# Values of branch B carried by the 512-column products of branch A in a hybrid attention encoder layer

## The chip, the cores and the metric

The kernel runs on one core of a Trainium2 chip. A core has a tensor engine (PE; its weight loads are listed apart as PEld), a vector engine (DVE), a scalar engine (ACT), a GpSimd engine (POOL) and a sync engine (SP) that here only issues DMAs; ACT and POOL issue DMAs too. Each works through its own instruction stream in order and waits on semaphores for the others. The metric is the device time of one execution in microseconds; the figure for a kernel is the median of its runs.

## The reference

One encoder layer is applied to two inputs with the same weights: `x_prompt` of 1024 tokens and `x_sample` of 512, both with a model width of 1024. Branch A is grouped-query attention (8 query heads, 2 key/value heads, 64 wide, queries and keys normalised and rotated), branch B neighbourhood attention on a token grid (8 heads, 64 wide).

```python
z = xn @ w_in                     # xn = rmsnorm(x) * g
qa, ka, va, qb, kb, vb, ga, gb = jnp.split(z, idx, axis=-1)   # 512,128,128,512,512,512,1024,1024
qa = rope(rmsnorm(qa, q_norm_g)); ka = rope(rmsnorm(ka, k_norm_g))
o_a = gqa_attention(qa, ka, va)
o_b = neighbourhood_attention(qb, kb, vb, rpb)
merged = sigmoid(ga) * (o_a @ w_proj_a) + sigmoid(gb) * (o_b @ w_proj_b)
h = x + merged @ w_out
y = rmsnorm(h + relu(rmsnorm(h) @ w_mlp_up)**2 @ w_mlp_down)
```

All is float32. The columns that matter here are `qa` (0 to 512), `ka` (512 to 640), `va` (640 to 768) and `vb` (1792 to 2304) of `w_in`.

## The kernel before

**Precision by three products.** A float32 product is made of three products of a faster type. Every operand is split into a high part (an ACT copy into that type) and a low part (a DVE subtraction of the copy from the source); `split` (L182 to L191) does it for weights, and `mm3` (L194 to L197) multiplies high by high, high by low and low by high into one accumulator. A product over the 1024 rows of the weights takes eight blocks of 128 rows, so 24 matrix instructions per 128 tokens.

**Two trunks, one after the other.** Trunk 0 is `x_sample` (4 token tiles of 128, `first` is true), trunk 1 is `x_prompt` (8 token tiles). In each trunk a loop over `g` (0 and 1), the head groups of branch A, runs a projection stage `phR` and an attention stage `phA`; then come branch B, the output projection and the MLP, which hold most of the time.

**The projection stage.** For each token tile `tt`:
- product `z`: 384 columns, which are the 256 of four query heads of group g, 64 of its key head and 64 of its value head. Its weights come from `load_a(g)` (L456): two loads of 512 KB for the queries, one raw tile for keys and values, split into `wh` and `wl`, tiles of 4 x 384 columns. The very first tile of trunk 0 is multiplied in two parts, 256 and 128 columns.
- `values(tt - 2)` (L606): product `zv` of 256 columns, the values of four heads of branch B (heads 0 to 3 with g = 0, 4 to 7 with g = 1). ACT copies the high part to `vt`, DVE subtracts the low part (L616, L617), and a DMA from ACT's queue stores 256 KB to `vd` in memory (L620), from where branch B gathers its key rows later. The weights `wv` come from `load_v(g)`, two loads of 512 KB; those for g = 1 are loaded and split during the attention stage of g = 0.
- `heads_t(tt - 2)` (L585): three transposes by PE (L590) of the rotated query and key heads `rr`; ACT and DVE write the high and low parts into `qT` and `kT` (L594 to L599).
- `chain(tt)` (L623): ACT squares the five heads (L629, into a scratch tile `sq`) and copies the value's high part (L630); DVE makes the mean (L176); POOL takes the power (L180); DVE the value's low part (L632) and the scaled heads `t` (L637); POOL `u` (L645); DVE `t` (L651) and `rr` (L653), with one head of `rr` on POOL (L654).

With g = 0 the token tiles are also normalised and transposed in this stage (`xn`, `ptxs`, L260 to L306). The tiles `z` and `zv` are made in accumulators of one pool; `raw` tiles, in which weights land before they are split, come from a pool of their own, and SP issues their loads in order, each waiting for its tile to come free.

**The tail of a projection stage** (after the last `z`): `values(NT - 2)`, `heads_t(NT - 2)`, `values(NT - 1)`, six steps of `fill.pull`, `heads_t(NT - 1)`. `fill` is a store of matrix work with no urgent reader, the gate products `gpss` of 512 columns: one step is three matrix instructions. The attention stages draw from the same store between their own instructions.

**Order.** Within a stage a scheduler orders the instructions of each engine; `keep_in_program_order` pins some. The stages follow one another in the order written.

Of the kernel before, what the change touches and what calls it, by code (L numbers as in the profile page):

```python
# [18 lines left out]
P = 128  # L19
# [42 lines left out]
def encoder(ctx: ExitStack, tc: tile.TileContext, xs, outs, w):  # L62
# [333 lines left out]
    def run(tr, nxt, first):  # L396
# [59 lines left out]
        def load_a(g, between=None, then=None, last=None):  # L456
            wh, wl, rq = [], [], []
            for kb in range(2):
                wh.append(slot([P, 4, 384], F32R, f"wgh{N}_{g}_{kb}"))
                wl.append(slot([P, 4, 384], F32R, f"wgl{N}_{g}_{kb}"))  # L460
                raw = rawp.tile([P, 1024], F32, tag="raw", name=f"rawq{N}_{g}_{kb}")
                rv = raw.rearrange("p (k c) -> p k c", c=256)
                nc.sync.dma_start(
                    rv,
                    win[kb * 512 : (kb + 1) * 512, 256 * g : 256 * g + 256].rearrange("(k p) c -> p k c", p=P),
                )
                rq.append(rv)
# [9 lines left out]
            for i, off in enumerate((512 + 64 * g, 640 + 64 * g)):  # L477
                nc.sync.dma_start(
                    rv[:, :, 64 * i : 64 * i + 64],
                    win[:, off : off + 64].rearrange("(k p) c -> p k c", p=P),  # L480
                )
            if last is not None:
                last()
            for kb in range(2):
                split(
                    wh[kb][:, :, 256:384],
                    wl[kb][:, :, 256:384],
                    rv[:, kb * 4 : kb * 4 + 4, :],
                    between is not None,
                )  # L490
            return wh, wl

        def load_v(g, alloc, pin=False, hold=None):
            return load_cols(win, 1792 + 256 * g, 256, f"v{N}_{g}", alloc, pin, hold)

        early = {}
        for g in range(2):
            with phase(f"phR{N}_{g}") as ph:
                xn_of, pre = {}, {}
                fresh = g == 0 and tr.ready < NT  # L500
                if fresh and not first:

                    def shape(tag):
                        bufs, dims, dt = {
                            "vt": (2, [P, 4, P], F32R),
                            "sq": (1, [P, 5, HD], F32),
                            "rt": (3, [P, 2, HD], F32),
# [5 lines left out]

                    pre = {tag: shape(tag) for tag in ("vt", "sq", "rt", "t", "u", "rr")}
                    gb = ph.tile([P, 1, D], F32, tag="gb", name=f"gb{N}", bufs=1)
# [52 lines left out]
                if g == 0 and first:  # L568
                    setup_tables()
                if early:  # L570
                    wv = early.pop("v")
                elif fresh and not first:
                    wv = load_v(g, lambda s_, d_, n_: room.pop(0))
                else:
                    wv = load_v(g, lambda s_, d_, n_: ph.tile(s_, d_, tag="wv", name=n_, bufs=2), first and fresh, held)
                qT = [slot([P, 2, T], F32R, f"qT{N}_{g}_{i}") for i in range(2)]
# [29 lines left out]
                def values(tt):  # L606
# [5 lines left out]
                    for k in range(NC8):  # L612
# [6 lines left out]
                    pending.append(  # L619
                        lambda: nc.scalar.dma_start(vd[tt * P : (tt + 1) * P, 4 * g : 4 * g + 4, :], vt.bitcast(F32))  # L620
                    )

                def chain(tt, z, rt):  # L623
                    nm = f"{N}_{g}_{tt}"
                    sq = pre.pop("sq", None) or ph.tile([P, 5, HD], F32, tag="sq", name=f"sq{nm}", bufs=1)
                    zq = z[:, :320].rearrange("p (h d) -> p h d", d=HD)
                    ss = sml.tile([P, 8], F32, tag="ss", name=f"ssA{nm}")
                    for i in range(5):
                        nc.scalar.activation(sq[:, i, :], zq[:, i, :], AF.Square, accum_out=ss[:, i : i + 1])  # L629
                    nc.scalar.activation(vhl[:, tt, 0:HD], z[:, 320:384], AF.Copy)  # L630
                    r = rstd(ss[:, :5], 5, HD, f"A{nm}")
                    nc.vector.tensor_tensor(  # L632
                        vhl[:, tt, HD:P], z[:, 320:384], vhl[:, tt, 0:HD].bitcast(F32), op=ALU.subtract
                    )
                    t = pre.pop("t", None) or ph.tile([P, 5, HD], F32, tag="t", name=f"t{nm}", bufs=2)
                    for i in range(5):
# [21 lines left out]
                for tt in range(NT):  # L658
# [18 lines left out]
                    if first and fresh and tt < 2:  # L677
                        tc.keep_in_program_order(op)
                    z = mm(f"z{nm}")[:, :384]
                    js = slice(j * P, (j + 1) * P)  # L680

                    for c0, c1 in ((0, 256), (256, 384)) if first and g + tt == 0 else ((0, 384),):
                        for k in range(NC8):
# [11 lines left out]
                    if tt >= 2:  # L695
                        values(tt - 2)
                        heads_t(tt - 2)
# [30 lines left out]
            with phase(f"phA{N}_{g}") as ph:  # L728
# [1067 lines left out]
```

## Time and profile before

| | us |
|---|---|
| three runs | 2144.89, 2145.60, 2146.26 (median 2145.6) |
| profiled execution | 2146.21, of which the traced span is 2144.4 |
| PE busy | 2115.7 (99% of the span) |
| DVE, ACT, POOL busy | 1474.8, 1112.1, 368.7 |
| phR of trunk 0, g = 0 and g = 1 | about 8 to 54 and 97 to 131 |
| phR of trunk 1, g = 0 and g = 1 | about 378 to 454 and 583 to 648 |

How to read the rows: `zs<-wghs,xs_0h` is an instruction that writes tile z from the weights wgh and the activations xs_0h (buffer numbers left out); L196 is the line of the kernel before. In the timeline the first number is the start in us from the beginning of the span, the second the duration; xN means N instructions put together, and a bracket at the end gives the idle time of the engine just before and what ended it. Matrix instructions overlap in the pipeline, so the pace of PE is read from start to start and not from durations. In the list of waits a row gives the engine and line that waited, what for, the us in total, how many times, and the longest. In the table by stage a row gives the stretch, its length, the busy us of PE, PEld, DVE, ACT and POOL with the number of instructions, PE's granted clock, the share of the DMA engines and GB/s.

### The profile page before, as it was taken

To read this page: it belongs to the slowest core of one execution; us is meant where nothing else is said; L and a number is where in the kernel's file an instruction comes from. 1 tells how busy PE (TensorE), PEld (TensorE's weight loads), DVE (VectorE), ACT (ScalarE), POOL (GpSimd) and SP (SyncE) were. 2 spreads that over 40 slices of the span, in tenths; PEclk is the share of its full clock that TensorE was granted. 3 is DMA by queue.
4 is the path that set the end of the run, shared out by engine and by line. 5 is a ranking of instruction groups with operands and counts; after the bars stand their busy time and mean duration, and the time that the engine had idled before them with its cause. 6 is when DMAs were issued, how large, how long until landed. Compare 5 with 4: busy or idle time off the path is not lost.

```text
span 2144.4 us, 32035 instructions
## 1 busy us (share of the span) xinstructions
PE 2115.7 (99%) x10967; PEld 1847.5 (86%) x10967; DVE 1474.8 (69%) x2889; ACT 1112.1 (52%) x2367; POOL 368.7 (17%) x470
## 2 busy tenths in 40 slices
PE   8999999999999999999999999999999999999998
PEld 7788778888898888887888899999999988888886
DVE  6675786877667755656882877777777777759563
ACT  5655654557646644555530566566655643434342
POOL 3232310433233223333200200003000000000000
PEclk9999999999999999999999999999999999999999
DMA  6437557520122133444472665578545799688561
GB/s 185 130 105 206 152 160 253 179 84 25 54 79 71 42 95 109 131 119 112 140 236 105 213 195 183 173 247 205 165 142 156 256 357 341 212 280 278 165 204 61
DMA packets 321258, 354.07 MB, mean 165 GB/s; under 512 B 31551, under 2 KB 255431, under 8 KB 321095
## 3 DMA queue, kind: packets, MB, share of 16 engines
q1 hardware_dynamic: 277927, 279.65, 41.8%
q10 hardware_dynamic: 36016, 52.19, 7.0%
q0 software_dynamic: 7152, 20.19, 3.5%
q8 instruction: 87, 1.43, 0.3%
q14 instruction: 76, 0.62, 0.1%
HBM read 264.85 MB, written 87.88 MB: 164 GB/s over the span
## 4 chain that ended last, share of the span: by engine, by line
PE 76%; DVE 1%; issue 0%; ACT 0%; POOL 0%; POOLq 0%; ACTq 0%; DVEq 0%
PE dn L196 6%; PE dn L197 6%; PE dn L195 6%; PE pTs L783 3%; PE gpss L195 3%; PE gpss L197 3%; PE gpss L196 3%; PE ua L197 2%; PE ua L195 2%; PE ua L196 2%; PE ud L195 2%; PE ud L197 2%; PE ud L196 2%; PE uc L197 2%; PE uc L195 2%; PE uc L196 2%
## 5 line engine op out<-in xcount | busy, mean ns | idle before, releaser
L197 PE MATMUL dn<-wd,al 128*128 128x512 f32 x624 | 242.8, 389 | 0.0
L196 PE MATMUL dn<-wd,ah 128*128 128x512 f32 x624 | 242.8, 389 | 0.0
L195 PE MATMUL dn<-wd,ah 128*128 128x512 f32 x624 | 242.7, 389 | 0.0
L1273 ACT ACTIVATE ah<-ar 128x512 fp32r<-128x512 f32 x168 | 104.3, 627 | 205.8 <-PE dn L196 183.6
L1274 DVE TENSOR_TENSOR al<-ar,ah 128x512 fp32r<-128x512 f32 x168 | 113.8, 685 | 77.8 <-ACT ah L1273 65.9
L195 PEld LDWEIGHTS dn<-wd,ah 128*128 128x128 f32 x624 | 117.1, 188 | 24.4
L196 PEld LDWEIGHTS dn<-wd,ah 128*128 128x128 f32 x624 | 117.1, 188 | 24.3
L197 PEld LDWEIGHTS dn<-wd,al 128*128 128x128 f32 x624 | 117.1, 188 | 24.2
L789 DVE TENSOR_TENSOR ptls<-pTs,pths 128x512 fp32r<-128x512 f32 x160 | 107.6, 686 | 37.9 <-ACT pths L788 37.0
L749 POOL TENSOR_SCALAR ps<-ps,rls 128x1024 f32<-128x1024 f32 (+1 forms) x96 | 97.1, 1012 | 212.6 <-DVE rls L748 192.1
L788 ACT ACTIVATE pths<-pTs 128x512 fp32r<-128x512 f32 x160 | 94.2, 598 | 73.8 <-PE pTs L783 71.6
L743 DVE TENSOR_REDUCE nms<-ss 128x1 f32<-128x1024 f32 (+1 forms) x96 | 99.8, 1041 | 25.3 <-PE ss L741 24.8
L195 PE MATMUL gpss<-xs_0h,w_gs 128*128 128x512 f32 x256 | 105.5, 412 | 0.5 <-DVE ot_Bs L440 0.4
L180 POOL TENSOR_TENSOR rs_f<-ms_f,mhalf 128x1 f32<-128x1 f32 x6 | 4.0, 667 | 590.7 <-DVE ms_f L176 590.7
L746 ACT ACTIVATE ps<-ss,nms 128x1024 f32<-128x1024 f32 (+1 forms) x96 | 93.3, 973 | 22.5 <-DVE nms L743 18.7
L783 PEld LDWEIGHTS pTs<-ident,ps 128*128 128x128 f32 x640 | 78.1, 140 | 28.2 <-POOL ps L749 4.3
L197 PE MATMUL gpss<-xs_0h,w_gs 128*128 128x512 f32 x256 | 101.1, 395 | 0.3 <-DVE w_gs L190 0.3
L196 PE MATMUL gpss<-xs_0l,w_gs 128*128 128x512 f32 x256 | 101.0, 394 | 0.0
L783 PE MATMUL pTs<-ident,ps 128*128 128x128 f32 x640 | 98.9, 274 | 1.3 <-DVE ptls L789 0.6
L1273 ACT ACTIVATE A<-S 128x512 fp32r<-128x512 f32 x128 | 75.8, 623 | 31.8 <-DVE S L1336 23.0
L957 POOL TENSOR_TENSOR bms<-rects,msks 128x384 f32<-128x384 f32 (+1 forms) x72 | 70.2, 978 | 128.7 <-DVE nmbs L974 107.5
L1274 DVE TENSOR_TENSOR A<-S,A 128x512 fp32r<-128x512 f32 x128 | 84.5, 686 | 4.1 <-ACT A L1273 4.1
(330 smaller groups left out, 6372.1 us busy)
## 6 DMA issues: line engine op xcount, KB each, us to landing
ar<-ud SPq DMA_DIRECT2D x120, 512.0 KB
br<-in_w_mlp_down_dram SPq DMA_DIRECT2D x72, 512.0 KB
rawu<-in_w_mlp_up_dram SPq DMA_DIRECT2D x64, 512.0 KB
ud<-c ACTq DMA_DIRECT2D x128, 192.0 KB
raw_gs<-in_w_in_dram SPq DMA_DIRECT2D x32, 512.0 KB
zgs<-sgs ACTq DMA_DIRECT2D x48, 256.0 KB
ud<-cs SPq DMA_DIRECT2D x64, 192.0 KB
raw_os<-in_w_out_dram SPq DMA_DIRECT2D x16, 512.0 KB
```

Of the source, the lines that this page charges most:

```text
L195: nc.tensor.matmul(out, ah, bh, start=start, stop=False, **kw)
L196: nc.tensor.matmul(out, ah, bl, start=False, stop=False, **kw)
L197: nc.tensor.matmul(out, al, bh, start=False, stop=stop, **kw)
L743: nc.vector.tensor_reduce(nm_, s, axis=AX.X, op=ALU.max, negate=True)
L746: nc.scalar.activation(p, s, AF.Exp, bias=nm_, accum_out=l)
L749: nc.gpsimd.tensor_scalar(p, p, rl, 1.0, op0=ALU.mult, op1=ALU.mult)
L783: nc.tensor.transpose(pt[:, j * P : (j + 1) * P], PP[u, j][:, kc * P : (kc + 1) * P], ident)
L788: nc.scalar.activation(hi, pt, AF.Copy)
L789: nc.vector.tensor_tensor(lo, pt, hi.bitcast(F32), op=ALU.subtract)
L957: nc.gpsimd.tensor_tensor(bm.rearrange("p (r c) -> p r c", c=32), rects[h][:, ir : ir + kr_n, jr : jr + 32], msk[:, hf * 3 + ct, :].rearra ...
L1273: nc.scalar.activation(hi, src, AF.Copy)
L1274: nc.vector.tensor_tensor(lo, src, hi.bitcast(F32), op=ALU.subtract)
```

## The change

Each 512-column accumulator is filled: the product `z` gets 128 further columns, the values of two heads of branch B. With g = 0 these are heads 0 and 1, with g = 1 heads 6 and 7 (`VB`). The other four heads (2 to 5) are made by `values`, once per trunk, in the stage of g = 0.

- `load_a` loads and splits a fourth piece (128 columns, 512 KB, `rawvb`), so `wh` and `wl` are 512 wide. In the first call it gets a slot of its own; in the other calls it takes a raw tile.
- `load_v` is called once per trunk. The load and split of value weights in the attention stage of g = 0 is gone; the fourth piece of `load_a(1)` is loaded there.
- `chain` copies and subtracts the two value heads into `vz` (one buffer with g = 0, two with g = 1) and stores 128 KB from ACT's queue. Its squares are written into `t` instead of a scratch tile.
- The first tile's two parts are 256 and 256 columns.
- The tail with g = 0 is as before. With g = 1, where there are no `values`, three steps of gate products stand ahead of `heads_t(NT - 2)` and six ahead of `heads_t(NT - 1)`.

```diff
         def load_a(g, between=None, then=None, last=None):
...
-                wh.append(slot([P, 4, 384], F32R, f"wgh{N}_{g}_{kb}"))
-                wl.append(slot([P, 4, 384], F32R, f"wgl{N}_{g}_{kb}"))
+                wh.append(slot([P, 4, 512], F32R, f"wgh{N}_{g}_{kb}"))
+                wl.append(slot([P, 4, 512], F32R, f"wgl{N}_{g}_{kb}"))
...
+            raw = raw_tile(f"rawvb{N}_{g}") if between is None else slot([P, 1024], F32, f"rawvb{N}_{g}", True)
+            rb = raw.rearrange("p (k c) -> p k c", c=P)
+            off = 1792 + HD * VB[g]
+            op = nc.sync.dma_start(rb, win[:, off : off + P].rearrange("(k p) c -> p k c", p=P))
+            if between is not None:
+                tc.keep_in_program_order(op)
...
+            for kb in range(2):
+                split(
+                    wh[kb][:, :, 384:512],
+                    wl[kb][:, :, 384:512],
+                    rb[:, kb * 4 : kb * 4 + 4, :],
+                    between is not None,
+                )
             return wh, wl

-        def load_v(g, alloc, pin=False, hold=None):
-            return load_cols(win, 1792 + 256 * g, 256, f"v{N}_{g}", alloc, pin, hold)
+        def load_v(alloc, pin=False, hold=None):
+            return load_cols(win, 1792 + 2 * HD, 256, f"v{N}", alloc, pin, hold)
+        VB = (0, 6)
...
-                            "sq": (1, [P, 5, HD], F32),
+                            "vz": (1, [P, 2, P], F32R),
...
-                if early:
-                    wv = early.pop("v")
-                elif fresh and not first:
-                    wv = load_v(g, lambda s_, d_, n_: room.pop(0))
-                else:
-                    wv = load_v(g, lambda s_, d_, n_: ph.tile(s_, d_, tag="wv", name=n_, bufs=2), first and fresh, held)
+                if fresh and not first:
+                    wv = load_v(lambda s_, d_, n_: room.pop(0))
+                elif g == 0:
+                    wv = load_v(lambda s_, d_, n_: ph.tile(s_, d_, tag="wv", name=n_, bufs=2), first and fresh, held)
...
-                        lambda: nc.scalar.dma_start(vd[tt * P : (tt + 1) * P, 4 * g : 4 * g + 4, :], vt.bitcast(F32))
+                        lambda: nc.scalar.dma_start(vd[tt * P : (tt + 1) * P, 2:6, :], vt.bitcast(F32))
...
                 def chain(tt, z, rt):
-                    sq = pre.pop("sq", None) or ph.tile([P, 5, HD], F32, tag="sq", name=f"sq{nm}", bufs=1)
+                    t = pre.pop("t", None) or ph.tile([P, 5, HD], F32, tag="t", name=f"t{nm}", bufs=2)
...
-                        nc.scalar.activation(sq[:, i, :], zq[:, i, :], AF.Square, accum_out=ss[:, i : i + 1])
+                        nc.scalar.activation(t[:, i, :], zq[:, i, :], AF.Square, accum_out=ss[:, i : i + 1])
                     nc.scalar.activation(vhl[:, tt, 0:HD], z[:, 320:384], AF.Copy)
+                    vz = pre.pop("vz", None) or ph.tile([P, 2, P], F32R, tag="vz", name=f"vz{nm}", bufs=1 + g)
+                    zb = z[:, 384:512].rearrange("p (h d) -> p h d", d=HD)
+                    nc.scalar.activation(vz[:, :, 0:HD], zb, AF.Copy)
...
+                    nc.vector.tensor_tensor(vz[:, :, HD:P], zb, vz[:, :, 0:HD].bitcast(F32), op=ALU.subtract)
+                    flush()
+                    pending.append(
+                        lambda: nc.scalar.dma_start(
+                            vd[tt * P : (tt + 1) * P, VB[g] : VB[g] + 2, :], vz.bitcast(F32)
+                        )
+                    )
...
-                    z = mm(f"z{nm}")[:, :384]
+                    z = mm(f"z{nm}")
-                    for c0, c1 in ((0, 256), (256, 384)) if first and g + tt == 0 else ((0, 384),):
+                    for c0, c1 in ((0, 256), (256, 512)) if first and g + tt == 0 else ((0, 512),):
...
-                        values(tt - 2)
+                        if g == 0:
+                            values(tt - 2)
                         heads_t(tt - 2)
...
-                values(NT - 2)
-                heads_t(NT - 2)
-                values(NT - 1)
-                fill.pull(6)
-                heads_t(NT - 1)
+                for tt in (NT - 2, NT - 1):
+                    if g == 0:
+                        values(tt)
+                    fill.pull(6 if tt == NT - 1 else 3 * g)
+                    heads_t(tt)
                 flush()
...
                         if g == 0 and ui == 1:
                             early["a"] = load_a(1)
-                        if g == 0 and ui == 2:
-                            early["v"] = load_v(1, slot)
```

More of the change, by code (lines that the diff above doesn't have):

```diff
@@ L512, in shape @@
                         return ph.tile(dims, dt, tag=tag, name=f"{tag}{N}_0", bufs=bufs)
-                    pre = {tag: shape(tag) for tag in ("vt", "sq", "rt", "t", "u", "rr")}
+                    pre = {tag: shape(tag) for tag in ("vt", "vz", "rt", "t", "u", "rr")}
                     gb = ph.tile([P, 1, D], F32, tag="gb", name=f"gb{N}", bufs=1)
@@ L634, in chain @@
                     )
-                    t = pre.pop("t", None) or ph.tile([P, 5, HD], F32, tag="t", name=f"t{nm}", bufs=2)
+                    nc.vector.tensor_tensor(vz[:, :, HD:P], zb, vz[:, :, 0:HD].bitcast(F32), op=ALU.subtract)
[5 more added lines that the diff above has]
+                    )
                     for i in range(5):
```

## The prediction

> **What bounds the kernel now.** I read the page first, then a table by stage, then the timeline of the tensor engine at both ends of each stage that the change touches. From the page:
>
> ```profile
> span 2144.4 us, 32035 instructions
> PE 2115.7 (99%) x10967; PEld 1847.5 (86%) x10967; DVE 1474.8 (69%) x2889; ACT 1112.1 (52%) x2367; POOL 368.7 (17%) x470
> PEclk9999999999999999999999999999999999999999
> ```
>
> The tensor engine (PE) is busy almost throughout and its clock is full, so only two things can move the time: how long PE's own work takes, and the 29 us in which it stands. By stage (busy time of PE, PEld, DVE, ACT, POOL in that order): the projection stages phR of trunk 0 are the first and third row, those of trunk 1 the last two; the second row is the attention between the first two.
>
> ```profile
> 8.00:54.00 46.00, 41.10 (x278) 38.40 (x278) 33.19 (x83) 24.12 (x81) 15.18 (x20) 1.00 0.61 169
> 54.00:97.00 43.00, 41.97 (x209) 32.34 (x208) 32.66 (x67) 30.81 (x65) 11.94 (x16) 1.00 0.46 138
> 97.00:131.00 34.00, 34.00 (x226) 32.98 (x224) 19.09 (x57) 13.41 (x63) 11.26 (x16) 1.00 0.33 107
> 378.00:454.00 76.00, 73.01 (x489) 69.58 (x487) 58.30 (x151) 42.11 (x157) 30.00 (x43) 1.00 0.51 163
> 583.00:648.00 65.00, 65.00 (x436) 63.50 (x435) 37.85 (x117) 26.43 (x127) 22.14 (x32) 1.00 0.29 91
> ```
>
> With g = 0 PE stands for 4.9 us (46.00 − 41.10) and 3.0 us (76.00 − 73.01); with g = 1 it never stands. So work added to g = 0 may fall into holes, and work taken from g = 1 is a gain only as long as what the work covered is not laid bare.
>
> **PE's work: the pace.** The change streams the same columns in 288 fewer products: 384 + 256 per token tile and head group become 512 + 256 with g = 0 and 512 with g = 1. What that is worth is read from start to start in the timeline of PE, first and last row of unbroken runs of products: 23 of 384 columns, 24 of 256, 13 of 512 and 21 of 128:
>
> ```profile
> 419.52 0.34 PE L196 MATMUL zs<-wgls,xs_1h 128*128 128x384 f32 x1
> ...
> 423.34 0.33 PE L197 MATMUL zs<-wghs,xs_1l 128*128 128x384 f32 x1
> ```
>
> ```profile
> 117.30 0.28 PE L195 MATMUL zvs<-wh_vs,xs_0h 128*128 128x256 f32 x1
> ...
> 120.05 0.28 PE L197 MATMUL zvs<-wh_vs,xs_0l 128*128 128x256 f32 x1
> ```
>
> ```profile
> 127.74 0.39 PE L197 MATMUL gpss<-xs_0h,w_gs 128*128 128x512 f32 x1
> ...
> 130.46 0.39 PE L197 MATMUL gpss<-xs_0h,w_gs 128*128 128x512 f32 x1
> ```
>
> ```profile
> 16.48 0.28 PE L195 MATMUL zs<-wghs,xs_0h 128*128 128x128 f32 x1
> ...
> 18.71 0.28 PE L197 MATMUL zs<-wghs,xs_0l 128*128 128x128 f32 x1
> ```
>
> That is 3.82/22 = 0.1736 us for 384 columns, 2.75/23 = 0.1196 for 256, 2.72/12 = 0.2267 for 512 and 2.23/20 = 0.1115 for 128. A tile with g = 0 gains 24 x (0.2267 − 0.1736) = +1.27 us of PE work; one with g = 1 loses 24 x (0.1736 + 0.1196 − 0.2267) = −1.60. Over a pair that is −0.32 (24 x 0.0131), and for the 12 token tiles of both trunks −3.8 us. The first tile of all is made in two parts; its second goes from 128 to 256 columns, which costs 24 x (0.1196 − 0.1115) = +0.2 instead of +1.27, so another −1.1. Together **−4.9 us**. [...]
>
> **PE's holes, trunk 0, g = 0.** The chain of waits, PE's rows alone, from 0 to 56 us and then from 372 to 456 us:
>
> ```profile
> PE pqs L590 <- DVE rrs L653: 3.0, 2, 1.6
> ...
> PE ptxs L290 <- DVE xns L266: 1.3, 2, 0.9
> ```
>
> ```profile
> PE ptxs L290 <- DVE xns L277: 1.6, 1, 1.6
> PE ptxs L290 <- DVE ms_s L176: 0.6, 1, 0.6
> PE zs L196 <- DVE wgls L190: 0.4, 1, 0.4
> ```
>
> In trunk 0 PE waits 4.3 us (3.0 + 1.3) for work of DVE on a token tile that it feeds itself. The +4.0 us of g = 0 (3 x 1.27 + 0.2) come ahead of these waits, while the chains behind them are paced by DVE, ACT and POOL. So I let the wider products fill most of them. Not all: the fourth weight piece (the 128 value columns) adds two ACT copies and four DVE subtractions ahead of the second half of the first tile. I take **−3.6**. Bounds: 0 (each chain starts as much later as its product is longer) and −4.3.
>
> The new copy and subtraction of two value heads (128 columns) cost ACT and DVE less per tile than the old 256-column pair does; with g = 0 there are both, with g = 1 the wide pair is gone. There the store of 128 KB goes out of a single buffer, so ACT's next copy stands until the store before it has landed. The tiles' squares are ahead of that copy on ACT, so the chain of the same tile isn't behind it; the transposed heads' copies are, with a tile period of 9.5 us to spare in trunk 1 (eight tiles in the 76 us of the table). Nothing is taken for it. Squares written into t wait for the sum of the tile two before; that is two tile periods back and nothing is taken either.
>
> **The ends of g = 1.** Here the change takes cover away. After the last product z the tensor engine had three stretches of value products, two groups of transposes and 18 gate products before it needed the last tile's rotated heads. The value products from 117.30 on, above, are the first such stretch in trunk 0. The row that ends this cover in trunk 0, then rows of ACT and DVE in it, then PE and DVE in trunk 1:
>
> ```profile
> 130.69 0.49 PE L590 MATMUL pqs<-ident,rrs 128*128 128x128 f32 x3
> ```
>
> ```profile
> 118.30 2.01 ACT L184 ACTIVATE w_gs<-raw_gs 128x1024 fp32r<-128x1024 f32 x2 [2.97 <-DVE vts L617]
> ```
>
> ```profile
> 119.37 3.70 DVE L190 TENSOR_TENSOR w_gs<-raw_gs,w_gs 128x512 fp32r<-128x512 f32 x6
> ...
> 124.44 1.05 DVE L637 SCALAR_TENSOR_TENSOR ts<-zs,rs_As,gtab 128x64 f32<-128x64 f32 x5 [1.03 <-POOL rs_As L180]
> ...
> 128.36 0.49 DVE L653 TENSOR_TENSOR rrs<-ts,us 128x320 f32<-128x320 f32 x1
> ```
>
> ```profile
> 632.21 0.28 PE L195 MATMUL zvs<-wh_vs,xs_1h 128*128 128x256 f32 x1
> ...
> 645.60 0.49 PE L590 MATMUL pqs<-ident,rrs 128*128 128x128 f32 x3
> ```
>
> ```profile
> 632.41 3.70 DVE L190 TENSOR_TENSOR w_gs<-raw_gs,w_gs 128x512 fp32r<-128x512 f32 x6
> ...
> 641.84 0.49 DVE L653 TENSOR_TENSOR rrs<-ts,us 128x320 f32<-128x320 f32 x1
> ```
>
> From the end of z to the last transposes there were 13.4 us of PE work in both trunks (130.69 − 117.30; 645.60 − 632.21), of which three value stretches of 24 x 0.1196 are 8.6. The last chain took 11.6 and 10.1 us (128.36 + 0.49 − 117.30; 641.84 + 0.49 − 632.21). After the change 9 + 18 gate products (27 x 0.2267 = 6.1 us) and two groups of transposes (0.25 each) are left, about 6.6 us. The chain loses the value copies and subtractions between its links (0.4 us each), and in trunk 0 ACT's wait of 2.97 us for one of them ahead of the gate splits; but the gate weights' 3.70 us on DVE stay ahead of its mean. I put it at 8.9 and 9.5 us: stalls of **+2.3** and **+2.9**. Bounds: 0 each (the splits already through: what the chain itself needs, at some eight steps of 0.5 to 1.2 us each, is inside 6.6) and +5.0 and +3.5 (nothing shorter). The nine gate products pulled forward are missing at the end of the attention behind; **+0.6** for both trunks, bounds 0 and 2.
>
> **The start of trunk 1.** The rows of SP, PE, DVE, PE again and ACT, and from the DMA view between 372 and 390 us the loads and stores of the same size, with their median time from issue to landing:
>
> ```profile
> 378.11 1.59 SPq L223 DMA_DIRECT2D raw_vs<-in_w_in_dram  x2
> ```
>
> ```profile
> 380.67 0.51 PE L195 MATMUL zs<-wghs,xs_0h 128*128 128x384 f32 x2
> ```
>
> ```profile
> 383.16 1.08 DVE L190 TENSOR_TENSOR wgls<-rawkvs,wghs 128x256 fp32r<-128x256 f32 x3
> ```
>
> ```profile
> 383.63 0.44 PE L196 MATMUL zs<-wgls,xs_0h 128*128 128x384 f32 x1 [0.36 <-DVE wgls L190]
> ```
>
> ```profile
> 388.80 2.00 ACT L184 ACTIVATE wvs<-raw_vs 128x1024 fp32r<-128x1024 f32 x2
> ```
>
> ```profile
> hnd<-xnhs POOLq DMA_DIRECT2D x3, 512.0 KB, 3.7
> hd<-hs POOLq DMA_DIRECT2D x2, 512.0 KB, 4.7
> ```
>
> The first product already waits for the split of keys and values. The new fourth piece is the next load on SP's queue, issued where raw_vs was (378.11), so its bytes and those of raw_vs behind it move down by one raw buffer. I let it land at about 382.5 (3.7 to 4.7 us as the rows of 512 KB on POOL's queue), be copied by ACT to 383.9 and subtracted behind the keys' (to 384.24): the product can run from about 384.6 instead of 380.67, +4.0 less the 0.9 us that it stood anyway. Behind it PE stood 2.8 us with the transposes of the rows above and smaller waits; the longer product covers these: +3.1 − 2.8 = **+0.3**. Bounds: −2.8 (the piece is there in time) and +7 (below).
>
> **Attention of trunk 0.** It sheds the split of 256 value columns (2.00 us of ACT by the row of raw_vs, 4 x 0.62 of DVE by the rows of 3.70 us for six) and takes on half of that. PE stands 1.0 us there (43.00 − 41.97); **−0.5**, bounds 0 and −1.0.
>
> **Sum:** −4.9 − 3.6 + 2.3 + 2.9 + 0.6 + 0.3 − 0.5 = −2.9. The profiled execution took 2146.21 us (span 2144.4), 0.6 above the median of its three runs (2145.6), so 2143.3 there and, rounded, **2143 us** as a median. A change under 0.2% (4.3 us) can hardly be told from none here.
>
> **Rivals.**
> *The ends hold.* The gate splits are through before the last z ends, since the shorter g = 1 stage leaves DVE less of other work; then neither end stalls: −8.1, 2137.5 us. For it: DVE has 19 of 34 us of work there. Against: the six subtractions stood directly before the mean in both trunks.
> *The start of trunk 1 is late: slower.* The fourth piece waits for a raw buffer as raw_vs did, and is split only where raw_vs is, at 388.80. Then the first product runs from about 390.7 (1.3 us of ACT, 0.6 of DVE), 10 us late, less 0.9 and the 2.8 behind it: +6.3 instead of +0.3, a sum of +3.1, 2148.7 us. It is slower than before from a first product at about 387.5 on (384.6 + 2.9). If trunk 0's holes don't fill either (+3.6), 2152. Against: ACT stands idle from 381 to 385.
> *Pace without a gain.* If the 13 ns per product belong to the weight load and not to the product, a wider product pays them too: the −4.9 goes, the rest of the sum (+2.0) stays, 2147.5 us. Against: 0.1736 − 384/2400, 0.1196 − 256/2400 and 0.2267 − 512/2400 are all 0.013 (0.2267 − 0.1196 = 0.1071 for 256 columns more gives the 2400 per us). [...]
>
> **Chances.** My forecast 0.43, the ends hold 0.30, late start 0.15, no pace gain 0.12. Faster by over 0.2% (under 2141.3) is the second case and a fifth of the first, 0.38; slower (over 2149.9) is the third and a little, 0.17; 0.45 between. The likeliest case's own range is 2140.5 to 2146; the range over the cases is 2137 to 2150.
>
> **What would show it.** PE's rows: 10,115 products of the program instead of 10,403, z at 0.227 us from start to start; pqs no longer waiting for rrs with g = 0; a wait of pqs for rrs of 2 to 3 us ahead of the last transposes of each g = 1 (none would make the second rival right); in trunk 1 a wait of the first z for the fourth piece, about 3 us (over 8 the third). It would be wrong altogether if PE's busy time in the four stages fell by less than 3 us, or if ACT's single value buffer showed up as a wait that PE inherits.

## The result and the profile after

The changed kernel takes 2150.92 us (median of nine runs, 2150.38 to 2152.09) against 2145.76 (nine runs, 2144.89 to 2146.26): +5.2 us, a ratio of 1.0025 with a 95% interval of 1.0017 to 1.0034. The forecast was 2143 us with a range up to 2150. It is wrong by 8 us, and in direction.

The page of the changed kernel, and the row of its core (span and mean granted clock; the kernel before has 0.999 there):

```profile
span 2150.1 us, 31487 instructions
PE 2115.5 (98%) x10679; PEld 1824.0 (85%) x10679; DVE 1478.2 (69%) x2909; ACT 1113.6 (52%) x2383; POOL 369.3 (17%) x470
```

```profile
core 0: 2150.1 us, clock 0.996
```

PE's busy time is the same with 288 products fewer, and the clock is a little lower. The table by stage, over the same stretches as before:

```profile
8.00:54.00 46.00, 44.16 (x274) 39.11 (x274) 33.46 (x88) 25.40 (x86) 14.09 (x20) 1.00 0.66 186
54.00:97.00 43.00, 41.36 (x208) 32.14 (x207) 33.19 (x71) 29.45 (x65) 11.92 (x16) 1.00 0.46 136
97.00:131.00 34.00, 31.33 (x141) 24.79 (x139) 17.06 (x55) 14.76 (x65) 12.12 (x16) 1.00 0.32 104
378.00:454.00 76.00, 73.42 (x409) 63.72 (x408) 55.48 (x146) 39.82 (x153) 27.04 (x40) 0.96 0.49 158
583.00:648.00 65.00, 63.26 (x301) 51.95 (x300) 35.89 (x108) 27.42 (x132) 22.53 (x29) 1.00 0.17 50
```

The holes of trunk 0, g = 0 have shrunk from 4.9 to 1.8 us, as forecast; the two stages with g = 1, where PE never stood, now have 2.7 and 1.7 us in the same stretches; and the fourth row has a clock of 0.96.

To see where the time went I cut the timeline of PE at six marks (the last transposes of each projection stage, the first product of trunk 1, the end) and took from each stretch its products times the paces of the prediction (0.1115, 0.1196, 0.1736 and 0.2267 us; for other widths an estimate from these, columns ÷ 2400 + 0.013). What is left is time in which PE did not keep its pace.

| stretch up to | work before | work after | left over before | left over after | difference | forecast |
|---|---|---|---|---|---|---|
| end of phR, trunk 0, g = 0 | 40.9 | 44.9 | 12.0 | 8.9 | −3.1 | −3.6 |
| end of phR, trunk 0, g = 1 | 72.9 | 68.6 | 3.8 | 8.1 | +4.3 | +1.8 |
| first product of trunk 1 | 237.8 | 235.7 | 12.0 | 15.2 | +3.2 | +3.4 |
| end of phR, trunk 1, g = 0 | 68.3 | 78.5 | 4.0 | 3.6 | −0.4 | −2.8 |
| end of phR, trunk 1, g = 1 | 189.1 | 178.6 | 3.8 | 8.7 | +4.9 | +2.9 |
| end | 1474.3 | 1472.0 | 15.0 | 16.8 | +1.8 | +0.3 |
| sum | 2083.2 | 2078.2 | 50.5 | 61.2 | +10.7 | +2.0 |

(The forecast's −0.5 for the attention of trunk 0 is in the second row, its +0.6 for missing gate products half each in the third and last, its +3.1 and −2.8 for the start of trunk 1 in the third and fourth.) The work falls by 5.0 us, 4.9 in the forecast. It is counted at the forecast's own paces, so this says only that the products are the ones foreseen. That the wider z keeps its pace is in two rows of PE, twelve steps apart in one unbroken run: 2.72/12 = 0.2267 us.

```profile
420.45 0.39 PE L197 MATMUL zs<-wghs,xs_1l 128*128 128x512 f32 x1
...
423.17 0.39 PE L197 MATMUL zs<-wghs,xs_1l 128*128 128x512 f32 x1
```

The leftover rose by 10.7 us instead of 2.0.

The first two causes stand in the list of waits of PE, for 97 to 133 us and 590 to 655 us, then 376 to 392 (line numbers are each kernel's own: L605 and L677 are L590 and L653 of the kernel before):

```profile
PE pqs L605 <- DVE rrs L677: 3.2, 2, 2.3
```

```profile
PE pqs L605 <- DVE rrs L677: 5.0, 2, 3.3
```

```profile
PE zs L195 <- ACT wghs L184: 2.5, 1, 2.5
```

Both ends of g = 1 have two waits each, ahead of the last but one tile's transposes as well as the last's; before, there was none. The first product of trunk 1 stands for its weights. The third cause is in the timeline of PE after the longest of these waits; products of 512 columns follow one another at 0.427 us, and at 0.23 again from 655.59 on:

```profile
651.81 0.64 PE L605 MATMUL pqs<-ident,rrs 128*128 128x128 f32 x3 [3.30 <-DVE rrs L677]
652.10 0.78 PE L765 MATMUL ss<-kTs,qTs 128*128 128x512 f32 x1
...
653.10 0.63 PE L196 MATMUL gpss<-xs_1l,w_gs 128*128 128x512 f32 x1
653.52 0.63 PE L765 MATMUL ss<-kTs,qTs 128*128 128x512 f32 x1
...
655.59 0.40 PE L197 MATMUL gpss<-xs_1h,w_gs 128*128 128x512 f32 x1
655.82 0.39 PE L195 MATMUL gpss<-xs_1h,w_gs 128*128 128x512 f32 x1
```

In the table by stretches (the number after the five engines is the granted clock) the same is seen at the start of trunk 1:

```profile
382.00:384.00 2.00, 1.22 (x2) 0.50 (x2) 2.00 (x7) 1.15 (x2) 1.72 (x3) 0.61 1.07 400
384.00:386.00 2.00, 1.99 (x5) 1.60 (x6) 2.00 (x4) 0.75 (x1) 0.24 (x1) 0.50 0.79 277
386.00:388.00 2.00, 2.00 (x9) 1.70 (x8) 1.04 (x3) 1.44 (x4) 0.56 (x1) 0.50 1.01 369
388.00:390.00 2.00, 2.00 (x10) 1.69 (x9) 0.81 (x3) 1.32 (x3) 1.13 (x2) 0.69 1.05 313
```

The record of the granted clock has it at one half for 6.83 us there and for 3.41 us after 652; before, nowhere but behind the last products (its record begins at about 10 us). At half clock the same products are busy for longer (0.63 us instead of 0.39 in the rows of PE above); half of the two together, 5.1 us, would account for PE's busy time on the page falling by 0.2 us only. The waits ahead of the two stretches were of 2.5 and 3.3 us.

### The profile page after: what moved, and what is told of

Same layout as the page of the kernel before. It is cut to its first block, busy times and chain, and to the rows that moved or that the text cites. A ratio compares the mean times of both kernels' runs of the same rounds, so it can differ in the third digit from the quotient of the medians.

```text
span 2150.1 us, 31487 instructions
## 1 busy us (share of the span) xinstructions
PE 2115.5 (98%) x10679; PEld 1824.0 (85%) x10679; DVE 1478.2 (69%) x2909; ACT 1113.6 (52%) x2383; POOL 369.3 (17%) x470
## 4 chain that ended last, share of the span: by engine, by line
PE 68%; DVE 1%; ACT 0%; issue 0%; POOL 0%; POOLq 0%; DVEq 0%; ACTq 0%
PE dn L195 6%; PE dn L196 6%; PE dn L197 6%; PE ua L195 2%; PE ua L196 2%; PE ua L197 2%; PE ud L195 2%; PE ud L196 2%; PE ud L197 2%; PE uc L195 2%; PE uc L196 2%; PE uc L197 2%; PE gpss L195 2%; PE gpss L197 2%; PE gpss L196 2%; PE ops L196 1%
```

## The experiments

Theory: the loss comes from cover taken from the ends of g = 1, from the fourth weight piece at the start of trunk 1, and from the half clock that follows such waits. Rivals: the wide products themselves lower the clock or save nothing; the single value buffer and the squares in t hold the chains; the waits only move. All edits are to the changed kernel unless the kernel before is named. The kernel before was timed along with each group: 2145.67 in the first, 2145.52, 2145.91, 2145.85 and 2145.67 in those that follow; in the order of the table the groups are four, four, three, one and two runs.

| run | us | ratio to before (95% interval) |
|---|---|---|
| changed kernel | 2150.92 | 1.0025 (1.0017 to 1.0034) |
| e_busy_gaps | 2148.82 | 1.0014 (1.0005 to 1.0024) |
| e_parts | 2149.39 | 1.0019 (1.0010 to 1.0029) |
| e_cover | 2144.89 | 0.9996 (0.9987 to 1.0005) |
| e_parts_cover | 2144.13 | 0.9993 (0.9984 to 1.0003) |
| e_busy_all | 2149.77 | 1.0021 (1.0011 to 1.0030) |
| e_slotr | 2151.17 | 1.0027 (1.0017 to 1.0037) |
| e_slotr_cover | 2145.39 | 1.0000 (0.9991 to 1.0010) |
| e_all_parts_cover | 2144.92 | 0.9999 (0.9990 to 1.0009) |
| e_before_tail | 2161.30 | 1.0071 (1.0054 to 1.0088) |
| e_fit | 2144.85 | 0.9994 (0.9985 to 1.0004) |
| e_lend | 2149.48 | 1.0016 (1.0007 to 1.0026) |
| e_before_tail2 | 2150.55 | 1.0022 (1.0013 to 1.0031) |
| e_start_busy | 2150.32 | 1.0021 (1.0012 to 1.0030) |
| e_cover_busy | 2144.01 | 0.9994 (0.9985 to 1.0003) |

### Cover at the ends

e_cover:

```diff
-                    fill.pull(6 if tt == NT - 1 else 3 * g)
+                    fill.pull(6 + 5 * g if tt == NT - 1 else 6 * g)
```

> In both trunks the tail of g = 1 gets 6 steps of gate products instead of 3 ahead of the transposes of the last but one tile, and 11 instead of 6 ahead of the last (24 products, 5.4 us more). Theory (the cover taken away at these ends costs stalls of 3.5 and 5.4 us and a half clock of 1.7): the waits of the transposes go, the attention behind gives back about a third of it; 4 to 8 us less than the changed kernel, 2143 to 2147. Rival (the gate products are only borrowed from the attention, which then stands instead): only the clock's 1.7 us come back, 2149.

2144.89 us, 6.0 less than the changed kernel. The waits of pqs are gone at both ends; the list of waits of PE from 97 to 136 us is empty. That is more than the whole loss of 5.2. With the waits goes half clock too: of its 6.83 and 3.41 us, 3.41 are left, at 384 (a clock of 0.55 from 384 to 386 us and 0.59 from 386 to 388). What was lent is given back in part in the attention: from 132 to 378 us, the list of waits of e_cover has the first row below; the kernel before has the second over the same stretch.

```profile
PE pTs L806 <- POOL ps L774: 2.6, 3, 1.9
```

```profile
PE pTs L783 <- POOL ps L749: 0.3, 1, 0.3
```

In the ledger above the stretch to the first product of trunk 1 has 18.3 us left over in e_cover, against 15.2 in the changed kernel.

e_lend goes further:

```diff
-                    fill.pull(6 if tt == NT - 1 else 3 * g)
+                    fill.pull(6 + 10 * g if tt == NT - 1 else 9 * g)
```

> The changed kernel with 9 and 16 steps of gate products at the ends of g = 1, 24 products per trunk more than the run with cover, where no wait is left to fill. Theory (the store of gate products is finite: what is lent is missing in the attention and in branch B): 1 to 4 us more than the run with cover, 2146 to 2149. Rival (the engine has work enough behind): the same as that run, 2144.5 to 2145.5.

2149.48 us, 4.6 more than e_cover and 0.5 above what was expected. Its waits of PE from 130 to 380 us:

```profile
PE pTs L806 <- POOL ps L774: 1.8, 3, 0.7
...
PE os L784 <- ACT pths L811: 0.8, 1, 0.8
PE ss L765 <- ACT ps L771: 0.7, 4, 0.2
PE os L784 <- DVE ptls L812: 0.7, 1, 0.7
```

The attention of trunk 0 runs out of gate products and waits for its own softmax. Its profiled execution, the fastest of ten (2147.07 us), has a mean granted clock of 0.999, that of the kernel before, so these rows show the kind of loss and not all of the median's. The other nine had 0.996 to 0.998 and took 2148.75 to 2150.63 us: a part of the 4.6 goes with a lower clock.

The other way round, the cover alone is taken from the kernel before. e_before_tail (short form; the tail is that of the changed kernel):

```diff
+                    if g == 1:
+                        values(tt)
                     z = mm(f"z{nm}")[:, :384]
...
                     if tt >= 2:
-                        values(tt - 2)
+                        if g == 0:
+                            values(tt - 2)
```

> The kernel before (384 and 256 columns, two buffers, own scratch for the squares), with one thing of the change alone: with g = 1 the value products of a tile are made ahead of its z instead of two tiles later, so that none is left for the tail, which gets the changed kernel's 3 and 6 steps of gate products. Theory (the loss is the cover taken from these ends): waits of the last transposes as in the changed kernel, 3.5 us in trunk 0 and 5.4 in trunk 1, half a clock after one or both, and 6 to 10 us more than the kernel before, 2152 to 2156. Rival (the loss comes from the wide products, the single value buffer or the squares in t): the time of the kernel before, 2146 to 2148.

2161.3 us (four runs), +15.4. That is more than the ends: in trunk 1 the first value product now also came ahead of its weights.

```profile
PE zvs L195 <- ACT wh_vs L184: 3.1, 1, 3.1
```

So it was made again with the value products one tile behind z (`values(tt - 1)` ahead of z for tt > 0, and ahead of the last z both that are left).

> As the last test on the kernel before, with the value products of g = 1 one tile behind z instead of ahead of it (the last tile's two ahead of its z), so that the first of them doesn't wait for its weights as it did there (3.1 us and a half-clock window). Theory (the loss is the cover taken from the ends of g = 1): waits of the last transposes of 2.5 to 3.6 us in each trunk and nothing new elsewhere, a half-clock window after one or both; 6 to 11 us more than the kernel before, 2152 to 2157. Rival (it was the misplaced start, and ends with little cover cost nothing): 2146 to 2148.

2150.55 us, +4.7 us (1.0013 to 1.0031) with nothing wide, no single buffer and squares in their own scratch. Its waits of PE from 97 to 136 and from 585 to 660 us:

```profile
PE pqs L590 <- DVE rrs L653: 1.1, 1, 1.1
```

```profile
PE pqs L590 <- DVE rrs L653: 1.6, 1, 1.6
```

The expectation was too high by 1.5 us and more: there is one wait at each end and not two (the last tile's two value products stand ahead of its z and cover the tile before it), and the mean granted clock of its profiled execution is 0.999, as in the kernel before. Yet the edit that only moves cover costs almost as much as the whole change. The ends are 2.7 us of it. Most of the rest lies behind them, where the nine gate products pulled into the tail are missing; over the whole span its waits of pTs have these rows, against 0.3 and 0.6 us in the kernel before:

```profile
PE pTs L787 <- POOL ps L753: 1.5, 3, 0.9
...
PE pTs L787 <- DVE ptls L793: 1.2, 3, 0.6
```

The rival that the wide products, the value buffer or the squares are to blame falls: a loss of this size comes without them, and e_cover, which has all three, is not slower than the kernel before.

### The start of trunk 1

e_parts:

```diff
-                    for c0, c1 in ((0, 256), (256, 512)) if first and g + tt == 0 else ((0, 512),):
+                    for c0, c1 in ((0, 256), (256, 512)) if g + tt == 0 else ((0, 512),):
```

> The first tile of trunk 1, too, is multiplied in two parts of 256 columns, so that its first 24 products need the query weights alone. Theory (the fourth weight piece is late, and costs a wait of 2.5 us and then the clock): the first product starts at about 380.1 instead of 382.75 and the clock stays full there; a wait of up to 1.5 us for the low part of the fourth piece moves into the second part; 4 to 5 us less than the changed kernel, 2146 to 2147. Rival (the wait only moves into the second part and the clock falls there): 2150 to 2151.

2149.39 us, 1.5 less: neither. The first product starts at 380.03 without a wait, but the list of waits from 376 to 426 us has a new one, of the next tiles' transposes:

```profile
PE ptxs L290 <- DVE ms_s L176: 1.5, 2, 1.1
PE zs L195 <- ACT wghs L184: 0.4, 1, 0.4
```

The edit takes away the product's wait of 2.5 us and gets 1.9 us in these rows instead. The waits of pqs at the end of g = 1 in trunk 1 are still there (5.1 us in two, from 600 to 652 us), and the mean granted clock of its profiled execution is 0.997, against 0.996 in the changed kernel and 0.999 in the kernel before.

e_slotr:

```diff
-            raw = raw_tile(f"rawvb{N}_{g}") if between is None else slot([P, 1024], F32, f"rawvb{N}_{g}", True)
+            raw = slot([P, 1024], F32, f"rawvb{N}_{g}", between is not None) if g == 0 else raw_tile(f"rawvb{N}_{g}")
```

> The fourth weight piece of trunk 1 gets a buffer of its own instead of a raw tile that has to come free. Theory (the wait of the first product is that of this load for its buffer): the load is issued at about 371 us instead of 377.5, the first product starts at about 380.1 without a wait, its clock stays full; 5 to 6 us less than the changed kernel, 2145 to 2146. Rival (the splits on ACT and DVE, not the load, hold the product): the start stays at 382 or later and no more than 1 us is won, 2150.

2151.17 us: the rival, in substance. The load goes out at 370.47 us instead of 377.48, as the row of SP shows, and the first product starts at 380.44, earlier than the rival had it; but the next one waits for the low part. Rows of SP, PE and DVE:

```profile
370.47 0.43 SPq L486 DMA_DIRECT2D rawvbs<-in_w_in_dram  x1
```

```profile
380.44 0.73 PE L195 MATMUL zs<-wghs,xs_0h 128*128 128x512 f32 x2 [0.84 <-ACT wghs L184]
383.39 0.79 PE L196 MATMUL zs<-wgls,xs_0h 128*128 128x512 f32 x1 [2.22 <-DVE wgls L190]
```

```profile
380.06 1.28 DVE L266 SCALAR_TENSOR_TENSOR xnhs<-hs,rs_hs,gbms 128x1024 f32<-128x1024 f32 x1 [0.46 <-POOL rs_hs L180]
381.26 0.15 DVE L176 TENSOR_SCALAR ms_ns<-ssns 128x1 f32<-128x1 f32 x1
381.32 0.68 DVE L1222 TENSOR_TENSOR hs<-ops,xrs 128x512 f32<-128x512 f32 x1
381.92 1.08 DVE L190 TENSOR_TENSOR wgls<-rawkvs,wghs 128x256 fp32r<-128x256 f32 x3
382.92 0.41 DVE L190 TENSOR_TENSOR wgls<-rawvbs,wghs 128x256 fp32r<-128x256 f32 x1
```

The fourth piece's first subtraction stands at the end of a queue on DVE that has the output projection's rows of trunk 0 in front. Two causes lie behind each other: with the late load removed, DVE's order holds the product as long.

The two edits combined with the cover:

> Both of the two edits before, the parts and the cover. Theory: their gains add up, 8 to 13 us less than the changed kernel, 2138 to 2143, faster than the kernel before, full clock throughout. Rival (the change gains nothing in the tensor engine's work, so that without its waits it equals the kernel before): 2146.

2144.13 us: 6.8 less than the changed kernel, short of the expected 8, with a mean granted clock of 0.999 in its profiled execution. It can't be told from the kernel before (0.9984 to 1.0003).

> The own buffer of the fourth piece, and 6 and 11 steps of gate products at the ends of g = 1. Theory: the first product's wait (2.7 us) and the one half-clock window (1.7) that the run with more cover still had go: 2140 to 2141.5, faster than the kernel before by 0.2%. Rival (what is won at the start is taken back by other waits behind it, as in the run with parts and cover): 2143.5 to 2144.5.

2145.39 us: the rival, and worse. The 2.2 us for DVE stay.

e_fit takes the parts, the own buffer and the cover, with 5 and 9 steps in trunk 0 instead of 6 and 11:

> The best parts together: own buffer for the fourth piece, first tiles in two parts, and cover at the ends measured to the waits: 5 and 9 steps in trunk 0, 6 and 11 in trunk 1. Theory (gate products lent to the tail are missing later, so only what fills a wait is worth lending; trunk 0 had 1.9 us of them too many): 0.5 to 2 us less than the run with parts and cover, 2142.5 to 2143.5. Rival (what is lent costs nothing, or the waits only move): 2144 to 2145.

2144.85 us (its kernel before 2145.91): the rival. In trunk 0, with less cover ahead of it, the wait moves on to the attention's second product, which needs the last tile's low keys:

```profile
PE ss L766 <- DVE kTs L612: 1.6, 1, 1.6
```

### The clock

e_busy_gaps puts products whose result is overwritten where PE stood:

```diff
+                    if not first and g + tt == 0:
+                        for _ in range(22):
+                            nc.tensor.matmul(z[:, 0:256], wh[0][:, 0, 0:P], wh[0][:, 0, 0:256], start=True, stop=True)
...
+                    for _ in range(spin):    # heads_t: 28 for the last tile of trunk 1, g = 1
+                        nc.tensor.matmul(pt[:, 0:2, :], wh[0][:, 0, 0:P], wh[0][:, 0, 0:256], start=True, stop=True)
```

> Adds products whose result is overwritten, where the tensor engine of the changed kernel stands: 22 of 256 columns (2.6 us) ahead of the first product of trunk 1, and 28 (3.3 us) ahead of the last transposes of its g = 1 stage. The waits behind them stay as they are. Theory (the clock halves because the engine stands): full clock throughout, no rows at 0.427 us from start to start, and 4.5 to 5 us less than the changed kernel, about 2146.2. Rival (the clock is lowered by the wider, denser products, not by standing): half clock again after each place, 2151 or a little more.

2148.82 us, 2.1 less. At both places the clock is 1.00 (380 to 392 and 650 to 658 us; the changed kernel's tables have 0.50 to 0.69 from 382 to 390 and 0.52 and 0.63 from 652 to 656), on the same products and behind the same chains; so there the half clock went with the standing and not with the products, and the rival falls. But in its profiled execution the clock fell to 0.57 in trunk 0 instead, after a wait of 2.3 us; behind one as long the changed kernel has 1.00 from 131 to 137 us:

```profile
131.00:133.00 2.00, 2.00 (x7) 1.57 (x6) 2.00 (x4) 0.83 (x3) 0.00 (x0) 0.57 0.22 49
133.00:135.00 2.00, 2.00 (x6) 1.59 (x6) 1.36 (x4) 0.00 (x0) 0.00 (x0) 0.57 0.00 0
```

e_busy_all fills all five gaps (9 and 21 products in trunk 0, 14 and 28 in trunk 1).

> As the run with products in two places, with products whose result is overwritten at all five: the first product of trunk 1 (22), and both last transposes of g = 1 in trunk 0 (9 and 21) and in trunk 1 (14 and 28). All waits stay. Theory: the clock stays full and what is left is the changed kernel less its half-clock time (4.7 us), 2146 to 2147, level with the kernel before. Rival (the clock falls on the wider stream, or the added products cost something of their own): 2149 or more.

2149.77 us: the clock is 1.00 from 380 to 392 and from 650 to 658 us and 0.999 in the mean, and still only 1.2 us come back. But the waits don't all stay. In the attention of trunk 0, PE now stands in two places where the changed kernel had 0.3 us in all; the rows are from 132 to 378 us:

```profile
PE ss L771 <- DVE kTs L614: 1.6, 1, 1.6
...
PE pTs L811 <- POOL ps L779: 1.1, 2, 0.9
```

From the last transposes of trunk 0 to the issue of the fourth piece's load it takes 2.1 us longer than the changed kernel (131.32 to 379.34, against 131.53 to 377.48). Two runs with the 22 products at the start of trunk 1 alone, in the changed kernel and in e_cover, were to tell the price:

> The changed kernel with overwritten products at one place only, 22 of 256 columns ahead of the first product of trunk 1. Theory (half clock costs its face: half of 6.8 us there): no half clock at 382 to 389, 2.5 to 3.4 us less than the changed kernel, 2147.5 to 2148.5. Rival (the stage behind is paced by DVE, ACT and POOL, so that a slower tensor engine there costs little): less than 1.5 us, 2149.5 to 2151.

> The run with more cover, whose only half clock was one window of 3.4 us at the first product of trunk 1, with the 22 overwritten products there. Theory (face price): 1 to 1.7 us less than that run, 2143.2 to 2144. Rival: the same, 2144.5 to 2145.

e_start_busy is at 2150.32 us, 0.6 less than the changed kernel, but does not decide: its profiled execution had a clock of 0.61 and 0.53 in the two stretches from 131 to 135 us and of 0.50 to 0.72 from 650 to 658, and ACT's split of the fourth piece came at 384.46 instead of 382.06. e_cover_busy is at 2144.01, 0.9 less than e_cover at the same time for the kernel before (2145.67).

The price is better read stretch by stretch in the profiled executions, where a moved wait elsewhere doesn't enter. From the first product of trunk 1 to the last transposes of that stage, e_cover takes 81.0 us (382.13 to 463.14) and e_cover_busy 79.4 (382.31 to 461.67): 1.6 less, nearly the 1.7 us that the 3.41 us of half clock in e_cover lose at their face (e_cover_busy has 1.00 from 380 to 388). The changed kernel takes 81.8 us there (382.75 to 464.59), with 3.4 us lost at face; e_busy_gaps 78.9 and e_busy_all 79.7. From the last transposes of g = 1 in trunk 1 to the end the three take 1498.3, 1497.4 and 1497.3 us, with 1.7 lost at face in the first. So of the changed kernel's 5.1 us (half of 6.83 + 3.41), some 3 to 4 reached the end in these single executions. That the medians give back only 1.2 and 2.1 fits the moved waits in the one and the half clock in trunk 0 in the other; it is not shown to be all of it.

### The price of a product

e_all_parts_cover multiplies every tile in two parts of 256 columns and is compared with e_parts_cover (shown is the main line; the work on the next token tile is put into the first part alone):

```diff
-                    for c0, c1 in ((0, 256), (256, 512)) if first and g + tt == 0 else ((0, 512),):
+                    for c0, c1 in ((0, 256), (256, 512)):
```

> The run with parts and cover, with all 24 tiles' products in two parts of 256 columns: 22 x 24 = 528 further products for the same columns. Theory (a product costs 13 ns whatever its width): 22 x 0.30 = 6.6 us more tensor work than the run with parts and cover, 3.6 us of it with g = 1, where nothing hides it; 4 to 6.6 us more time, 2148 to 2151. Rival (the number of products costs nothing): 2144, the same.

2144.92 us, 0.8 more than e_parts_cover, and 0.9 with the kernel before of each group taken into account (2145.52 and 2145.67). In the ledger the work rises by 6.6 us, as expected, and the leftover falls by about 3.9 (from 52.8 to 48.8). The ledger is of profiled executions, and that of e_all_parts_cover was one of its slow ones (2146.39); between those two the span grows by 2.6 us. By either figure, more than half of a product's 13 ns are not time: here, where the waits stand on chains of other engines, less PE work is more standing. The expected 4 us and more did not come.

## Why the prediction was wrong

**Pace.** Right as work: z runs at 0.2267 us from start to start, and the page has 288 products fewer (10,967 and 10,679; the prediction's 10,403 and 10,115 stand in no view). Wrong as time: the sum took the −4.9 whole. In e_all_parts_cover 6.6 us of such work moved the median by about 0.9, the profiled span by 2.6.

**The holes of trunk 0, g = 0.** Right: −3.6 forecast, −3.1 measured. PE's waits for rrs there are gone. The single value buffer did hold ACT in this stage, for 3.1 us in two waits for the store of vz; PE's list from 0 to 56 us has no wait for ACT, so PE inherited none that shows.

**Attention of trunk 0.** −0.5 forecast. In the stretch from 54 to 97 us PE stands for 1.6 us (43.00 − 41.36) where it stood for 1.0, so the term is not seen.

**The ends of g = 1.** The mechanism was right and the term mis-sized; it is the first failing step. "Stalls of +2.3 and +2.9" were a last chain of 8.9 and 9.5 us less 6.6 us of cover. The cover took some 7.4 us, but the chain, from the end of the last z to the last rr, took 10.5 us in trunk 0 (120.85 to 131.38) and 12.3 in trunk 1, and PE stood for 3.2 and 5.0 us, in two waits each. The prediction saw the gate weights on DVE ahead of the last mean. It did not see the tile before: with no value products between one z and the next, that tile is still in its own chain when the last z ends. Its rr stands ahead of the last mean too, and so do the low parts of keys and queries (kT, qT) of the tile before it. Rows of trunk 1, the last z and then DVE:

```profile
639.13 0.39 PE L197 MATMUL zs<-wghs,xs_1l 128*128 128x512 f32 x1
```

```profile
642.91 0.61 DVE L677 TENSOR_TENSOR rrs<-ts,us 128x320 f32<-128x320 f32 x1
643.44 1.88 DVE L190 TENSOR_TENSOR w_gs<-raw_gs,w_gs 128x512 fp32r<-128x512 f32 x3
645.25 0.28 DVE L612 TENSOR_TENSOR kTs<-pqs,kTs 128x128 fp32r<-128x128 f32 x1
645.54 0.86 DVE L614 TENSOR_TENSOR qTs<-pqs,qTs 64x256 fp32r<-64x256 f32 x2
646.43 0.17 DVE L176 TENSOR_SCALAR ms_As<-ssAs 128x5 f32<-128x5 f32 x1
...
651.17 0.49 DVE L677 TENSOR_TENSOR rrs<-ts,us 128x320 f32<-128x320 f32 x1
```

The last z ended at about 639.36 (its start and one pace), the mean came 7.1 us later and rr was done at 651.66. In the kernel before, the mean came 3.8 us after its z (632.21):

```profile
636.03 0.16 DVE L176 TENSOR_SCALAR ms_As<-ssAs 128x5 f32<-128x5 f32 x1
```

PE's first wait is not what lengthens the chain. In e_cover, where PE waits at neither place, it takes 12.4 us (637.65 to 650.03):

```profile
637.42 0.39 PE L197 MATMUL zs<-wghs,xs_1l 128*128 128x512 f32 x1
```

```profile
649.55 0.48 DVE L677 TENSOR_TENSOR rrs<-ts,us 128x320 f32<-128x320 f32 x1
```

The bounds of +5.0 and +3.5 held the first end and missed the second; with both of them the sum would have been +0.4.

**The start of trunk 1.** A wait of +3.1 forecast, 2.5 in the row of waits; right in size. That holes behind it would fill (−2.8) was right without the clock, and undone by it: −0.4, for the 3.6 us left over in that stretch hold about 3 of half clock (half of 6.83).

**The clock.** There was no term for it; the second failing step. I had two stalls of about 3 us in my own sum and read the clock's full row as a property of the kernel. Behind stalls of 2.5 and 3.3 us it was one half for 6.8 and 3.4 us. In the profiled stretches this cost 3 to 4 us; runs that fill the places gave back 1.2 and 2.1, with waits or half clock come in elsewhere. How it shares the 5.2 us with the ends stays open within these figures.

**Gate products pulled forward.** +0.6 forecast. e_cover and e_lend show what such a loan costs: the stretch behind it gives back 3 us, and beyond what fills a wait it is loss.

**The rivals.** "The ends hold" did not happen. "The start of trunk 1 is late" had the place, not the size: ACT split the piece at 382.06 and not at 388.80. Its times, 2148.7 and 2152 us, lie nearest to the measured one, and by luck: the product was 2 us late and not 10, and the ends and the clock, which make up the loss, are not in it. "Pace without a gain" gave 2147.5 on the condition that a wider product pays the 13 ns again; z at 0.2267 us shows that it does not. None had the ends themselves as the slower case.

No version found beats the kernel before by more than its measurement can tell; the best is e_parts_cover.

## What to carry to other kernels

When products on a saturated engine are merged or moved, ask first which chain they covered, and price that chain with everything that the tile before still has to do ahead of it on the same engine, since tiles that follow one another faster overlap there. A saved product is time only where nothing else waits there: set it against the stage's leftover, not against the span. Filler work taken from a store is a loan, and worth taking only for the wait that it fills.

## What was not expected of the hardware

Behind waits of PE of 2.2 to 3.4 us the granted clock was one half, for some 3.4 or 6.8 us: in the changed kernel for 6.83 us behind a wait of 2.5 and for 3.41 behind one of 3.3; by the tables by stretches for 6.8 behind one of 2.2 in e_slotr and for 3.4 behind 2.6 in e_cover, 2.3 in e_busy_gaps and each of 3.4 and 3.1 in e_before_tail.

The length of the wait alone did not decide it in these runs. A wait of 2.3 us in trunk 0 was followed by half clock in one execution (e_busy_gaps, 0.57 from 131 to 135 us) and not in another (the changed kernel, 1.00), one of 2.2 us at the start of trunk 1 was in e_slotr (0.50 from 384 to 388) and not in e_slotr_cover (0.999 in the mean, and products of 512 columns 0.23 us apart behind it). In e_before_tail2, with waits of 1.1 and 1.6 us, the mean was 0.999. What decides between two waits of one length was not shown.

The times of kernels with such waits scatter, and in these two runs they go with the mean granted clock of the execution: 2147.57 us at 0.998 and 2153.85 at 0.996 in e_parts, 2143.95 at 0.999 and 2147.44 at 0.997 in e_slotr_cover. The kernel before ran between 2145.08 and 2146.46 beside e_parts.
